# Turning table with its zero amid the chunks, output maps without power 0, and a new order of the S5 steps

## The chip, the cores and the metric

The kernel runs on one core of one Trainium2 chip. The metric is the device time of one execution in microseconds (us), from launch to the end; the number that counts is the median of several runs.

## What is computed

The reference is one step of a small hybrid encoder: two layers over 512 prompt rows and 32 sample rows of width 1024. Both layers end in a gated convolutional FFN. The change concerns the mixer of the first layer, an S5 state-space branch beside a cross-attention into 256 memory tokens:

```python
def s5_mixer(u, h0_re, h0_im, a_re, a_im, log_dt, b_re, b_im, c_re, c_im, d_skip, w_glu, b_glu):
    ...
    lam_re, lam_im = mag * jnp.cos(a_im * dt), mag * jnp.sin(a_im * dt)
    ...
    bu_re = jnp.einsum('blgc,gnc->blgn', ug, bb_re)
    bu_im = jnp.einsum('blgc,gnc->blgn', ug, bb_im)
    ...
    _, _, h_re, h_im = lax.associative_scan(
        _complex_affine_combine, (lam_re_t, lam_im_t, bu_re, bu_im), axis=1)
    y = (jnp.einsum('blgn,gcn->blgc', h_re, c_re.astype(f32))
         - jnp.einsum('blgn,gcn->blgc', h_im, c_im.astype(f32)))
    y = y.reshape(Bsz, L, MIX_IN) + d_skip.astype(f32) * u.astype(f32)
    y = jax.nn.gelu(y).astype(u.dtype)
    out = y * jax.nn.sigmoid(y @ w_glu + b_glu)
    return out, h_re[:, -1], h_im[:, -1]
```

There are 48 groups of 16 channels with 64 complex states each. The memory attention takes q from the same input gemm, normalises it over 64 columns, and attends to keys and values that a gemm over the memory tokens (prompt) or a cache (sample) gives.

## The kernel before

The kernel is one program with a fixed order on each of the five engines. Its blocks are written as Python functions, some as generators that are advanced by `unit(name, generator)`. A scheduler takes each block's instructions with a priority from the table ORDER (L63), and what comes out is the order in which each engine works, in sequence. Tiles come from free lists (Slots): a step that gets a tile waits until its last reader is done.

Large gemms are all in L324: fp32 operands split into a high and a low part, weights fetched by SP (L230), split by ACT into whi and wlo (L231, L232), and the low part is made by an accumulating DMA that POOL issues (L233).

The first layer goes through these stages, with times of the profile before:

- up to 69 us the input gemm (z0, L324 with ra and w_in), with the parameters of the S5 branch computed beside it in `s5_params`;
- from 69 to about 171 us the S5 stage in six chunks of 8 groups (128 channels);
- from 171 to 209 us the glu gemm (w_glu) with the memory attention between its six column blocks; then the rest of the kernel.

In the S5 stage eight time steps form a block, so that a sequence is 64 blocks (and 4 for the sample rows). For each chunk m:

- `s5_wv` (L671 on) makes on DVE the products that map inputs to states (L674, L676), `s5_wvt` transposes them on PE (L685);
- `s5_wc` (L693 on) makes on DVE the products of c and the powers of lambda (two L698 and their sum L700, each 128 x 1152: 8 groups, 9 powers, 16 channels). Powers 0 to 7 go with xq through 8 matmuls into the bank pk (L704), ACT evicts it into kp (L710), POOL adds the skip diagonal dd (L709, L711) and writes the block to DRAM (kd, L714);
- `s5_kernel` (L717 on) reads it back by eight DMAs of POOL (L723), each as a Toeplitz matrix, into two tiles kk;
- `s5_input` transposes the inputs of the chunk (PE L733, ACT L735, PE L743, ACT L744);
- `s5_scan` (L749 on) multiplies by wv on PE (L756), turns the phase by the table tab on DVE (L767 to L771), runs the real recurrence as a scan (L774; its factors `mul` and input `w` are prepared by ACT L760 and by the POOL memsets L761 and L763), turns back (L777), and forms hh (L783, L784). The table has 70 columns for each of 24 pairs of rows, real and imaginary part: powers 0 to 64 of the unit phase, and the columns 65 to 69 for the sample rows. It is built in `s5_params` by doubling (L640 to L650);
- `s5_output` multiplies u by kk (L795) and hh by powers 1 to 8 of wc (L796), evicts (ACT L800), transposes (PE L807), and applies the gelu (ACT L808, L809).

The loop over chunks (L1045 on) runs scan m, then the input and the products of chunk m+1, the output of chunk m-1, and at its end do_wc(m+1). Between them `fill` puts units of `mem_kv` (L337 on, matmuls L347), the gemm over the memory tokens, whose inputs have two tiles "rb" of their own. The memory attention `mem_attend` is a generator; its first part, norms of q and the sample rows' attention, runs ahead of the glu loop, and the others at blocks 1, 2, 4 and 5.

In the orders and rows below, rc is the split input of a gemm, bank a PSUM bank, fa, fx and big are tiles of the free lists (fx and big join late), and i_ names are inputs in DRAM.

Of the kernel before, what the change touches and what calls it, by code (L numbers as in the profile page):

```python
# [50 lines left out]
for _n, _w in (("mix", 2 * KD), ("bglu", NM), ("ffn", 2 * KD), ("kv", KD), ("mem", 2 * KD), ("ql", NM),  # L51
# [12 lines left out]
         "s5_input": 260, "norm0": 20, "s5_params": -50, "mem_attend0": 100, "s5_wc": 10, "q_front0": 10, "norm1": 0,  # L64
# [73 lines left out]
def body(ctx, tc, A, O):  # L138
# [5 lines left out]
    FW = 576  # L144
# [39 lines left out]
    warm = F.get(576)  # L184
# [3 lines left out]
    for _ in range(2):  # L188
        T.matmul(b, warm[:, 64:192], warm[:, 64:], start=True, stop=True)
# [227 lines left out]
    def mem_attend(l, zm, kv_p, kv_s, fm, bm, out):  # L417
        ktp, vp = kv_p
        kts, vs = kv_s
# [21 lines left out]
        r = rsqrt(x, 128, 17, "zr")  # L441
        mx, nm, su, ri = (sm(17, n) for n in ("zmx", "znm", "zsu", "zri"))
# [101 lines left out]
    def s5_params(pool, tmp, sp5):  # L544
# [121 lines left out]
        P.memset(q["kp"], 0.0)  # L666
        q["hf"] = pool.tile([128, NM, 8, 2], F32, name="hf")
# [377 lines left out]
    for m in range(NM):  # L1045
# [759 lines left out]
```

## Time and profile before

| what | before |
| --- | --- |
| median of 3 runs | 1437.56 us (1436.07 to 1439.15) |
| the profiled execution | 1436.17 us |
| its span, first to last instruction | 1434.4 us |
| PE busy | 1402.3 us (98%) |
| DVE busy | 714.6 us (50%) |
| ACT busy | 740.6 us (52%) |
| POOL busy | 385.7 us (27%) |
| mean granted clock of TensorE | 0.988 |

PE is the tensor engine, DVE the vector engine, ACT the scalar engine, POOL the general one, SP the one that issues DMAs. A busy PE can still work at half its clock: the column PEclk says which share of full speed was granted in a stretch. Idle time of the other engines costs nothing as long as PE does not wait for it. In the views, "[1.34 <-DVE wv L676]" behind a row says how long the engine stood before it and what released it.

### The profile page before, as it was taken

What the parts mean: (1) busy time and instruction counts of PE and PEld (TensorE: products, weight loads), DVE (VectorE), ACT (ScalarE), POOL (GpSimd) and SP (SyncE); (2) the same over time, 40 slices, a digit from 0 to 9 for tenths busy, and PEclk for the clock granted to TensorE, in tenths of its full rate; (3) what the DMA queues carried; (4) which work ended last, traced back from release to release, by engine and by line L of the source; (5) the groups of instructions that cost most, each with busy time, mean ns of one, the idle gap of its engine ahead of it and who ended that gap; (6) DMA issues with size and microseconds to landing.
All of it is one profiled execution on the core that took longest, in us unless ns stands there. A gap on an engine that the chain in (4) does not pass through costs nothing.

```text
span 1434.4 us, 26764 instructions
## 1 busy us (share of the span) xinstructions
PE 1402.3 (98%) x10661; PEld 1299.2 (91%) x10661; DVE 714.6 (50%) x1776; ACT 740.6 (52%) x1237; POOL 385.7 (27%) x668
## 2 busy tenths in 40 slices
PE   7999899999999999999989999999999999999998
PEld 6966689999999999999978986558999999999998
DVE  7999642555315541555357545663455514551351
ACT  6556464655435543555644554654565534553452
POOL 2065333222111211133336222332322211221121
PEclk8999899999999999999999999999999999999999
DMA  9443548788788888868741521103778887888775
GB/s 268 109 118 104 151 109 190 161 173 180 171 175 175 175 175 175 176 145 196 154 118 56 158 71 45 30 1 74 170 169 176 176 177 173 176 175 177 171 157 140
DMA packets 66045, 210.59 MB, mean 147 GB/s; under 512 B 9152, under 2 KB 11424, under 8 KB 65920
## 3 DMA queue, kind: packets, MB, share of 16 engines
q0 software_dynamic: 29152, 96.61, 37.4%
q1 hardware_dynamic: 35616, 110.17, 26.6%
q10 hardware_dynamic: 1152, 2.10, 0.4%
q8 instruction: 84, 1.38, 0.4%
q14 instruction: 41, 0.34, 0.1%
HBM read 203.22 MB, written 5.61 MB: 146 GB/s over the span
## 4 chain that ended last, share of the span: by engine, by line
PE 87%; DMA 4%; DVE 3%; ACT 2%; issue 2%; POOL 1%; SPq 0%; ACTq 0%; DVEq 0%; POOLq 0%
PE bank L324 67%; PE bank L1312 2%; PE bank L1560 2%; PE bank L1399 2%; PE bank L1596 1%; DMA wlo<-i_w_in 1%; PE bank L1513 1%; PE bank L1487 1%; PE bank L1585 1%; PE bank L347 1%; DMA wlo<-i_w_f 1%; PE bank L1201 1%; PE bank L479 1%; PE bank L1427 1%; PE bank L517 1%
## 5 line engine op out<-in xcount | busy, mean ns | idle before, releaser
L324 PE MATMUL bank<-rc,whi 128*128 128x272 f32 x3728 | 625.3, 289 | 0.2 <-DVE rc L305 0.2
L324 PEld LDWEIGHTS bank<-rc,whi 128*128 128x128 f32 x3728 | 528.2, 188 | 4.2 <-issue 3.1
L324 PE MATMUL bank<-rc,wlo 128*128 128x272 f32 x1864 | 388.3, 288 | 0.5 <-DMA wlo<-i_w_in 0.3
L231 ACT ACTIVATE whi<-wraw 128x1024 fp32r<-128x1024 f32 (+2 forms) x178 | 182.9, 1028 | 354.3 <-issue 304.0
L324 PEld LDWEIGHTS bank<-rc,wlo 128*128 128x128 f32 x1864 | 293.2, 188 | 1.3 <-DMA wlo<-i_w_in 0.5
L324 PE MATMUL bank<-g,whi 128*128 128x272 f32 x1408 | 234.8, 288 | 0.8 <-ACT g L216 0.8
L324 PEld LDWEIGHTS bank<-g,whi 128*128 128x128 f32 x1408 | 198.9, 188 | 1.4 <-ACT g L216 1.2
L233 POOL DMA_DIRECT2D wlo<-i_w_f x136 | 116.7, 858 | 303.9 <-ACT wlo L232 302.5
L232 ACT ACTIVATE wlo<-wraw 128x1024 fp32r<-128x1024 f32 (+2 forms) x178 | 180.6, 1015 | 0.6 <-PE bank L1513 0.5
L324 PE MATMUL bank<-g,wlo 128*128 128x272 f32 x704 | 145.6, 288 | 2.1 <-DMA wlo<-i_w_f 2.1
L855 DVE SCALAR_TENSOR_TENSOR fa<-fa,gp,fa 128x546 f32<-128x546 f32 x88 | 69.6, 791 | 139.6 <-ACT fa L854 139.6
L869 DVE TENSOR_TENSOR h<-bank,h 128x272 f32<-128x272 f32 x96 | 38.2, 435 | 173.2 <-PE bank L324 172.6
L324 PEld LDWEIGHTS bank<-g,wlo 128*128 128x128 f32 x704 | 110.3, 188 | 2.5 <-DMA wlo<-i_w_f 2.5
L854 ACT ACTIVATE fa<-fa,gp 128x546 f32<-128x546 f32 x88 | 73.1, 831 | 12.5 <-DVE fa L849 12.5
L847 DVE TENSOR_TENSOR fa<-bank,fa 128x272 f32<-128x272 f32 x88 | 38.9, 442 | 80.5 <-PE bank L324 76.7
L856 DVE SCALAR_TENSOR_TENSOR fa<-fa,gp,fa 128x546 f32<-128x546 f32 x88 | 69.5, 790 | 3.1
L895 ACT ACTIVATE fa<-fa 128x546 f32<-128x546 f32 x44 | 29.1, 662 | 71.7 <-DVE fa L856 71.7
L851 POOL COPY fa<-gp 128x2 f32<-128x2 f32 x88 | 19.9, 227 | 170.2 <-DVE g L217 107.9
L852 POOL COPY fa<-fa 128x4 f32<-128x4 f32 x88 | 18.2, 207 | 164.5 <-DVE fa L849 164.5
L324 PE MATMUL bank<-ra,whi 128*128 128x272 f32 x256 | 47.7, 309 | 2.7 <-ACT whi L241 2.7
L216 ACT ACTIVATE g<-fa 128x544 fp32r<-128x544 f32 x44 | 28.9, 658 | 37.6 <-DVE fa L897 37.6
L896 DVE TENSOR_TENSOR fa<-fa,fa 128x512 f32<-128x512 f32 x44 | 30.5, 693 | 33.5 <-ACT fa L895 33.5
(628 smaller groups left out, 1987.2 us busy)
## 6 DMA issues: line engine op xcount, KB each, us to landing
wraw<-i_w_f SPq DMA_DIRECT2D x120, 512.0 KB, 4.9
wlo<-i_w_f POOLq DMA_DIRECT2D x120, 512.0 KB, 7.4
wraw<-i_w_out SPq DMA_DIRECT2D x16, 512.0 KB, 4.4
wlo<-i_w_out POOLq DMA_DIRECT2D x16, 512.0 KB, 7.0
wraw<-i_w_in SPq DMA_DIRECT2D x14, 512.0 KB, 5.1
wlo<-i_w_in POOLq DMA_DIRECT2D x14, 512.0 KB, 7.5
wraw<-i_w_f SPq DMA_DIRECT2D x16, 384.0 KB, 3.1
wlo<-i_w_f POOLq DMA_DIRECT2D x16, 384.0 KB, 5.9
```

The lines of the kernel that those rows point to most:

```text
L216: S.activation(hi, src, AF.Copy)
L231: S.activation(hi, raw, AF.Copy)
L232: S.activation(lo, raw, AF.Copy, scale=-1.0)
L233: P.dma_start(lo, ap, accum_op=ALU.add)
L324: T.matmul(ps[q][:, :c], ww, xx[:, c0:c0 + c], start=k == 0 and i == 0, stop=k == n - 1 and i == 2)
L847: V.tensor_tensor(u[:, 2:274], ps[0][:, :272], rb[:, :272], ALU.mult)
L854: S.activation(y, u[:, 2:548], AF.Identity, scale=gcol("cw", 3 * ci + 2), bias=gcol("cb", ci))
L855: V.scalar_tensor_tensor(y, u[:, 1:547], gcol("cw", 3 * ci + 1), y, ALU.mult, ALU.add)
L856: V.scalar_tensor_tensor(y, u[:, 0:546], gcol("cw", 3 * ci), y, ALU.mult, ALU.add)
L869: V.tensor_tensor(h[m][:, c0:c0 + cc], ps[qd][:, :cc], h[m][:, c0:c0 + cc], ALU.add)
L895: S.activation(yg, yg, AF.Silu)
L896: V.tensor_tensor(u[:, 2:514], ya[:, :NP], yg[:, :NP], ALU.mult)
```

## The change

The table tab gets its zero turn at column 32 of 70. Powers 0 to 32 are built by doubling in six levels where there were eight; the 32 columns to the left are two reversed copies by ACT, the imaginary one with sign -1. A scan turned by a constant phase more or less gives the same states, so nothing else of it changes. The products wc hold powers 1 to 8 alone (128 x 1024), and power 0 of the kernel block comes from cc by a matmul of its own (16 columns, L710) beside that of powers 1 to 7 (112 columns, L711). The skip diagonal is computed once for all chunks (L670). do_wc(m+1) stands behind scan m and its first fill. mem_attend yields after the norms of q; that part runs in iteration 3 of the loop, the others at glu blocks 1 to 5, with priority 30 for the name mem_attend0 where 100 stood. FW goes from 576 to 560, the tiles tb and wc from 1152 columns to 1024, the two tiles rb of mem_kv fall away (it takes from F), and the order in which two tile sets join F is swapped.

```diff
-         "s5_input": 260, "norm0": 20, "s5_params": -50, "mem_attend0": 100, "s5_wc": 10, "q_front0": 10, "norm1": 0,
+         "s5_input": 260, "norm0": 20, "s5_params": -50, "mem_attend0": 30, "s5_wc": 10, "q_front0": 10, "norm1": 0,
...
-    FW = 576
+    FW = 560
...
         r = rsqrt(x, 128, 17, "zr")
+        if early:
+            yield
+        (ktp, vp), (kts, vs) = kv_p, kv_s() if early else kv_s
...
-        for o, lvl, c0, n in ((1, 0, 0, 1), (2, 1, 0, 2), (4, 2, 0, 4), (8, 3, 0, 8), (16, 4, 0, 16), (32, 5, 0, 16),
-                              (48, 5, 16, 16), (64, 6, 0, 1)):
+        for o, lvl, c0, n in ((1, 0, 0, 1), (2, 1, 0, 2), (4, 2, 0, 4), (8, 3, 0, 8), (16, 4, 0, 16), (32, 5, 0, 1)):
...
-        V.tensor_copy(view(tab, [[70, 2 * NPR], [1, 5]], 65), view(tab, [[70, 2 * NPR], [1, 5]]))
-
-        prd = pool.tile([128, 2, 9, 48], F32, name="prd")
+        for i, s in ((0, 1.0), (1, -1.0)):
+            S.activation(tab[:, i, :, 0:32], view(tab, [[70, NPR], [-1, 32]], SR * i + 64), AF.Copy, scale=s)
+        S.activation(view(tab, [[70, 2 * NPR], [1, 5]], 65), view(tab, [[70, 2 * NPR], [1, 5]], 32), AF.Copy)
+
+        prd = pool.tile([128, 2, 8, 48], F32, name="prd")
...
+        q["dd"] = pool.tile([128, 2 * NM, 16], F32, name="dd")
+        P.tensor_tensor(q["dd"], view(cn, [[0, 2 * NM], [1, 16]], 128), view(q["dsk"], [[1, 2 * NM], [0, 16]]), ALU.mult)
...
-        c, d = fd.get(8, 9, 16), fb.get(8, 9, 16)
+        c, d = fd.get(8, 8, 16), fb.get(8, 8, 16)
...
-                T.matmul(pk[32 * i:32 * i + 32, 128 * gh:128 * gh + 128],
-                         view(q["xq"], [[1, 32]], 16 * (8 * m + 4 * gh + i)),
-                         c[:, 4 * gh + i, 0:8].rearrange("p a b -> p (a b)"), start=True, stop=True)
+                x, g = view(q["xq"], [[1, 32]], 16 * (8 * m + 4 * gh + i)), 4 * gh + i
+                o = pk[32 * i:32 * i + 32, 128 * gh:128 * gh + 128]
+                T.matmul(o[:, :16], x, q["cc"][:, 0, 8 * m + g], start=True, stop=True)
+                T.matmul(o[:, 16:], x, c[:, g, 0:7].rearrange("p a b -> p (a b)"), start=True, stop=True)
...
-    R, fx = slots(lr, 2, F32, 512, "rb"), slots(lr, 3, F32, FW, "fx")
-    FA, FB, FD = slots(lr, 2, F32, 1024, "wv"), slots(lr, 1, F32, 2 * FW, "tb"), slots(lr, 3, F32, 2 * FW, "wc")
+    fx = slots(lr, 3, F32, FW, "fx")
+    FA, FB, FD = slots(lr, 2, F32, 1024, "wv"), slots(lr, 1, F32, 1024, "tb"), slots(lr, 3, F32, 1024, "wc")
     fxs = list(fx.free)
+    F.merge(Slots([big[:, FW * i:FW * i + FW] for i in range(4)]))
     F.merge(fx)
-    F.merge(Slots([big[:, FW * i:FW * i + FW] for i in range(4)]))
...
-    mkv = mem_kv(F, R, BG, BS, (kvp, (mk1, mv1)))
+    mkv = mem_kv(F, F, BG, BS, (kvp, (mk1, mv1)))
...
         fill(fills[m][0])
         if m < NM - 1:
+            do_wc(m + 1)
             g_in = s5_input(zts[m + 1], F, BS)
...
-        if m < NM - 1:
-            do_wc(m + 1)
+        if m == 3:
+            unit("att_norms", att)
...
-        if m in (1, 2, 4, 5):
+        if m:
             unit("mem_attend0", att)
```

What this does to the engines' orders is shown at three places. The first is POOL at the start, beside the input gemm. Before:

```order
L242 TENSOR_TENSOR wlo_100<-wraw_94,whi_97 128x512
L709 TENSOR_TENSOR fa_76<-cn,sp_145 128x32
L233 DMA wlo_101<-i_w_in 128x1024
L763 MEMSET fa_72 128x8
L233 DMA wlo_99<-i_w_in 128x1024
L233 DMA wlo_100<-i_w_in 128x1024
L761 MEMSET fa_79 128x8x2
```

After:

```order
L242 TENSOR_TENSOR wlo_100<-wraw_94,whi_97 128x512
L670 TENSOR_TENSOR dd<-cn,sp_145 128x192
L765 MEMSET fa_79 128x8
L233 DMA wlo_101<-i_w_in 128x1024
L233 DMA wlo_99<-i_w_in 128x1024
L233 DMA wlo_100<-i_w_in 128x1024
L763 MEMSET fa_78 128x8x2
```

The memset of the first scan's w moved from behind the first of the three weight DMAs to ahead of it, and its tile is another one.

The second place is DVE around the products of wc for the last chunk (wc_868 before, wc_862 after). Before, they stand behind the hh of scan 4 (L783, L784) and ahead of scan 5 (L767):

```order
L676 TENSOR_TENSOR wv_864<-wv_864,tb_865 128x1024
L783 TENSOR_TENSOR big<-fa_91,fa_86 64x280
L784 TENSOR_TENSOR big<-fa_91,fa_86 64x280
L783 TENSOR_TENSOR big<-fa_91,fa_86 64x280
L784 TENSOR_TENSOR big<-fa_91,fa_86 64x280
L698 TENSOR_TENSOR wc_868<-cc_399,prd 128x1152
L698 TENSOR_TENSOR tb_865<-cc_399,prd 128x1152
L217 TENSOR_TENSOR rc_1767<-fa_80,rc_1766 128x544
L700 TENSOR_TENSOR wc_868<-wc_868,tb_865 128x1152
L767 TENSOR_TENSOR fa_74<-bank_63,tab 128x4x69
```

After, they stand among the hh of scan 3 (L785, L786), and scan 4 (L769) begins ten rows behind these:

```order
L702 TENSOR_TENSOR wc_862<-cc_399,prd 128x1024
L785 TENSOR_TENSOR fa_92<-fa_75,fa_78 64x280
L786 TENSOR_TENSOR fa_92<-fa_75,fa_78 64x280
L785 TENSOR_TENSOR fa_92<-fa_75,fa_78 64x280
L786 TENSOR_TENSOR fa_92<-fa_75,fa_78 64x280
L702 TENSOR_TENSOR tb_859<-cc_399,prd 128x1024
L678 TENSOR_TENSOR wv_858<-bb_395,pr_397 128x1024
L704 TENSOR_TENSOR wc_862<-wc_862,tb_859 128x1024
L436 TENSOR_SCALAR zx_0_1479<-bank_70 128x17
L678 TENSOR_TENSOR tb_859<-bs_396,pi_398 128x1024
```

The products of the last chunk moved one scan forward, and the norms of q (L436) came in behind them.

The third place is POOL around the last kernel block (kd_394) and its reload. Before:

```order
L763 MEMSET fx_860 128x8
L355 TENSOR_TENSOR fx_862<-fx_862,fa_79 128x512
L233 DMA wlo_101<-i_w_glu 128x768
L711 TENSOR_TENSOR kp<-kp,big 128x2x16
L714 DMA kd_394<-kp 128x480
L430 MEMSET fa_73 128x256
L723 DMA fa_92<-kd_394 128x1x128 x4
L723 DMA fa_72<-kd_394 128x1x128 x4
L233 DMA wlo_99<-i_w_glu 128x768
```

After:

```order
L788 COPY hf<-fa_92 128x16
L714 TENSOR_TENSOR kp<-kp,dd 128x2x16
L716 DMA kd_394<-kp 128x480
L355 TENSOR_TENSOR big<-big,fa_78 128x512
L725 DMA fa_74<-kd_394 128x1x128 x4
L725 DMA fx_856<-kd_394 128x1x128 x4
L788 COPY hf<-fa_79 128x16
L763 MEMSET big 128x8x2
L765 MEMSET fa_91 128x8
L233 DMA wlo_101<-i_w_glu 128x768
```

The block's write and reload moved ahead of the memsets of the last scan and of the first weights of the glu gemm.

## Rows read from the trace of the kernel before

**Rows 1.** Windows: stretch, length; busy PE, PEld, DVE, ACT, POOL; PEclk, DMA share, GB/s

```profile
69.00:140.00 71.00, 66.76 (x608) 46.79 (x607) 68.62 (x100) 39.02 (x101) 42.87 (x73) 0.98 0.37 109
140.00:150.00 10.00, 9.42 (x66) 6.15 (x64) 8.87 (x27) 3.13 (x7) 3.68 (x5) 1.00 0.67 175
150.00:160.00 10.00, 5.61 (x27) 4.69 (x28) 6.04 (x23) 5.91 (x16) 7.95 (x13) 0.61 0.66 136
160.00:171.38 11.38, 11.24 (x62) 7.29 (x60) 5.19 (x24) 6.89 (x17) 1.73 (x3) 0.80 0.45 159
```

**Rows 2.** Waits of PE, 69 to 171.38 us: released by; total us, times, longest

```profile
PE bank L795 <- DMA fa<-kd: 2.5, 2, 1.7
PE bank L807 <- ACT big L800: 2.5, 1, 2.5
PE bank L685 <- DVE wv L676: 1.3, 1, 1.3
...
PE bank L704 <- DVE wc L700: 0.7, 1, 0.7
```

**Rows 3.** Chain that ended last, at the S5 stage's end: start, us, what

```profile
144.18 6.59 DMA kd<-kp
...
151.66 4.71 DMA fa<-kd
```

**Rows 4.** Timeline of DVE: start, us, line, out<-in [idle before <-releaser]

```profile
124.73 0.45 DVE L767 TENSOR_TENSOR fa<-bank,tab 128x276 f32<-128x276 f32 x1
...
139.19 1.35 DVE L700 TENSOR_TENSOR wc<-wc,tb 128x1152 f32<-128x1152 f32 x1
...
150.33 0.45 DVE L784 TENSOR_TENSOR fa<-fa,fx 64x280 f32<-64x280 f32 x1
```

**Rows 5.** Groups of DVE by form, 69 to 140 us: count, busy us, mean ns

```profile
L698 DVE TENSOR_TENSOR tb<-cc,prd 128x1152 f32<-128x1152 f32 x5 | 6.8, 1351 | 0.0
...
L674 DVE TENSOR_TENSOR tb<-bs,pi 128x1024 f32<-128x1024 f32 x4 | 4.9, 1226 | 0.0
```

**Rows 6.** Timeline of ACT near the S5 stage's end

```profile
150.16 0.84 ACT L231 ACTIVATE whi<-wraw 128x768 fp32r<-128x768 f32 x1 [3.46 <-DMA wraw<-i_w_glu]
```

**Rows 7.** Timeline of DVE, a table level of 16 columns

```profile
53.61 0.96 DVE L646 TENSOR_TENSOR big<-tab,p_sc 128x768 f32<-128x768 f32 x1
54.48 0.95 DVE L647 TENSOR_TENSOR big<-tab,p_sc 128x768 f32<-128x768 f32 x1
...
56.62 0.55 DVE L648 TENSOR_TENSOR tab<-big 128x384 f32<-128x384 f32 x1
57.09 0.55 DVE L649 TENSOR_TENSOR tab<-big 128x384 f32<-128x384 f32 x1
```

**Rows 8.** Timeline of PE, small matmuls

```profile
23.11 0.24 PE L262 MATMUL bank<-cn,fa 128*32 128x1 f32 x8
23.29 0.39 PE L324 MATMUL bank<-ra,whi 128*128 128x272 f32 x1
...
71.82 0.65 PE L704 MATMUL bank<-wc,xq 128*32 128x128 f32 x16
```

**Rows 9.** DMA issues of the whole run: count, KB each, us to landing

```profile
kd<-kp POOLq DMA_DIRECT2D x6, 240.0 KB, 2.4
...
fa<-i_mem SPq DMA_DIRECT2D x3, 256.0 KB, 2.9
```

**Rows 10.** Groups of ACT by form, 155 to 175 us

```profile
L376 ACT ACTIVATE fa<-bank,mrs 128x256 f32<-128x256 f32 x2 | 1.0, 496 | 1.9 <-PE bank L347 1.9
```

**Rows 11.** Timeline of DVE and PE at the front

```profile
19.98 0.72 DVE L953 TENSOR_TENSOR fa<-fa,fa 128x544 f32<-128x544 f32 x1
...
27.20 0.82 PE L324 MATMUL bank<-ra,wlo 128*128 128x272 f32 x2 [3.14 <-DMA wlo<-i_w_in]
```

**Rows 12.** The chain at the front

```profile
19.26 7.89 DMA wlo<-i_w_in
```

**Rows 13.** Timeline of PE in the glu stage

```profile
187.80 0.66 PE L507 MATMUL bank<-cn,fa 128*128 128x128 f32 x4 [1.08 <-POOL fa L495]
```

More of the change, by code (lines that the diff above doesn't have):

```diff
@@ L183, in body @@
     h = [base.tile([128, NT], F32, name=f"h{k}") for k in range(KD)]
-    warm = F.get(576)
+    warm = F.get(560)
     V.memset(warm, 0.0)
@@ L188, in body @@
     for _ in range(2):
-        T.matmul(b, warm[:, 64:192], warm[:, 64:], start=True, stop=True)
+        T.matmul(b, warm[:, :128], warm[:, :512], start=True, stop=True)
     B.put(b)
@@ L414, in mem_cache, with mem_attend @@
         return kt, v
-    def mem_attend(l, zm, kv_p, kv_s, fm, bm, out):
-        ktp, vp = kv_p
-        kts, vs = kv_s
+    def mem_attend(l, zm, kv_p, kv_s, fm, bm, out, early=False):
         ps = bm.get(512)
@@ L637, in s5_params @@
         tab = pool.tile([128, 2, NPR, 70], F32, name="tab")
-        V.memset(tab[:, 0, :, 0:1], 1.0)
-        V.memset(tab[:, 1, :, 0:1], 0.0)
+        V.memset(tab[:, 0, :, 32:33], 1.0)
+        V.memset(tab[:, 1, :, 32:33], 0.0)
         SR = NPR * 70
-        for o, lvl, c0, n in ((1, 0, 0, 1), (2, 1, 0, 2), (4, 2, 0, 4), (8, 3, 0, 8), (16, 4, 0, 16), (32, 5, 0, 16),
-                              (48, 5, 16, 16), (64, 6, 0, 1)):
+        for o, lvl, c0, n in ((1, 0, 0, 1), (2, 1, 0, 2), (4, 2, 0, 4), (8, 3, 0, 8), (16, 4, 0, 16), (32, 5, 0, 1)):
             t0 = view(tmp, [[NPR * n, 2], [n, NPR], [1, n]])
             t1 = view(tmp, [[NPR * n, 2], [n, NPR], [1, n]], H)
-            src = view(tab, [[SR, 2], [70, NPR], [1, n]], c0)
+            src = view(tab, [[SR, 2], [70, NPR], [1, n]], 32 + c0)
             V.tensor_tensor(t0, src, view(sc, [[0, 2], [1, NPR], [0, n]], NPR * (lvl + 1)), ALU.mult)
             V.tensor_tensor(t1, src, view(sc, [[0, 2], [1, NPR], [0, n]], NPR * (8 + lvl + 1)), ALU.mult)
-            V.tensor_tensor(tab[:, 0, :, o:o + n], t0[:, 0], t1[:, 1], ALU.subtract)
-            V.tensor_tensor(tab[:, 1, :, o:o + n], t0[:, 1], t1[:, 0], ALU.add)
-        V.tensor_copy(view(tab, [[70, 2 * NPR], [1, 5]], 65), view(tab, [[70, 2 * NPR], [1, 5]]))
-        prd = pool.tile([128, 2, 9, 48], F32, name="prd")
+            V.tensor_tensor(tab[:, 0, :, 32 + o:32 + o + n], t0[:, 0], t1[:, 1], ALU.subtract)
+            V.tensor_tensor(tab[:, 1, :, 32 + o:32 + o + n], t0[:, 1], t1[:, 0], ALU.add)
+        for i, s in ((0, 1.0), (1, -1.0)):
+            S.activation(tab[:, i, :, 0:32], view(tab, [[70, NPR], [-1, 32]], SR * i + 64), AF.Copy, scale=s)
+        S.activation(view(tab, [[70, 2 * NPR], [1, 5]], 65), view(tab, [[70, 2 * NPR], [1, 5]], 32), AF.Copy)
+        prd = pool.tile([128, 2, 8, 48], F32, name="prd")
         xq = pool.tile([128, 49, 16], F32, name="xq")
@@ L795, in s5_output @@
                 T.matmul(o, u[:, 4 * gh + i, :], kk[gh][:, i], start=True, stop=False)
-                T.matmul(o, hh[:, 4 * gh + i, 0:69], wc[:, 4 * gh + i, 1:9].rearrange("p a b -> p (a b)"), start=False,
+                T.matmul(o, hh[:, 4 * gh + i, 0:69], wc[:, 4 * gh + i].rearrange("p a b -> p (a b)"), start=False,
                          stop=True)
@@ L1023, in fill @@
             nfill += 1
-    wvs = []
+    wvs, mo = [], []
+    att = mem_attend(0, zm, kvp, lambda: kvs, F, BS, mo, True)
     def products(m):
```

16 lines of the change are left out of this document (5 added, 11 removed).

## Prediction

> **What bounds the kernel now.** The profile's page gives PE 98% of the span, so a gain can only come from where PE stands still or runs slowly. The windows show where that is [rows 1]. From 69 to 140 us PE is busy 66.76 of 71.00 us at a clock of 0.98; the next ten are nearly full (9.42); from 150 to 160 us it is busy 5.61 of 10.00 at clock 0.61, and up to 171.38 us it is busy but at 0.80. Behind that lie the glu gemm and work that the change doesn't touch: behind the glu stage every engine's order is word for word the same. So the question is when the glu gemm starts, 171.38 us now.
>
> The list of waits says what PE stood on between 69 and 171.38 us [rows 2]: 2.5 us on the loads of the last chunk's Toeplitz tiles (DMA fa<-kd), 2.5 us on an ACT eviction (L800), 1.3 us on DVE's products (wv), 0.7 us on DVE's wc. The chain explains the first two [rows 3]: the last kernel block is written to DRAM at 144.18 us, lands 6.59 us later, and its reload takes 4.71 us more; the reload releases PE. The block is late because it is computed late: DVE ends the products of wc for chunk 5 at 140.54 us (139.19 + 1.35), after scan 4, and the last hh is ready at 150.78 (150.33 + 0.45) [rows 4]. Through the whole S5 stage it is DVE that sets the pace: 68.62 busy of 71.00 us [rows 1].
>
> The change acts on these two things, DVE's amount of work and the place of the wc step, and it adds small work on PE and moves waits on POOL and ACT.
>
> **A. The tail (minus 9.4).** do_wc(m+1) goes from the end of an iteration to right behind scan m. In DVE's order the three wc operations of chunk 5 leave the place behind scan 4 and stand with the hh of scan 3. From wc to reloaded tile takes 15.83 us now (140.54 to 156.37, [rows 3, 4]). In the new order scan 4 and scan 5 lie in between. From the first operation of scan 4 (124.73) to the last hh (150.78) are 26.05 us now [rows 4], of which the three wc operations that leave are 4.0 (1351 ns each, [rows 5]), so some 22 us are left and the reload lands 6 us before hh needs it, even at the slow 6.59. The 2.5 us on DMA then go. The 2.5 us on L800 go too: L800 stood on ACT behind an L231 that waited 3.46 us for its weights at 150.16 us [rows 6]; in ACT's new order the L231 of the first two glu weights stand ahead of the evictions of chunk 4, not between those. That makes 5.0 us of waits. The clock is priced from the windows: (1 - 0.61) x 5.61 + (1 - 0.80) x 11.24 = 2.2 + 2.2 = 4.4 us [rows 1], lost in a stretch in which PE stood still again and again; what still waits behind the last hh I count under D. Ends: 0 (the reload comes late all the same) and -9.4. I take -9.4.
>
> **B. DVE's work (minus 5.7).** The table loses two levels of 16 columns: four products at a step of 0.87 us (53.61 to 54.48) and four sums at 0.47 (56.62 to 57.09), 5.4 us [rows 7]. The 18 wc operations shrink from 1152 to 1024 columns: L698 takes 1351 ns and L674, the same kind on 1024, 1226 [rows 5], 18 x 0.125 = 2.3. Together -7.7; the table's copy of five columns goes to ACT besides. Added ahead of the last hh is the query norm (eight operations on 17 columns and some copies: about 2 us, a guess, since the trace has them later and in the shadow of other work), so DVE is 5.7 us shorter. What this can give PE is what PE stood on in 69 to 150 us: 71.00 - 66.76 + 10.00 - 9.42 = 4.8 us, and (1 - 0.98) x 66.76 = 1.3 of clock, 6.1 [rows 1]. The smaller counts, -5.7. Ends 0 and -6.1. The two reversed copies of the table on ACT (128x768) lie beside the z0 gemm; without that cover they hold up the first scan, by no more than DVE's 0.87 for as many columns each [rows 7].
>
> **C. PE's new matmuls (plus 1.8).** Power 0 no longer lies in wc, so each of the 48 kernel products becomes two: 16 columns from cc and 112 from wc. L704's sixteen records, two for each product, take at most 0.65 us, 41 ns each; eight records of one column (L262) take 0.18 us (23.11 to 23.29), 22.5 ns each [rows 8]. 96 new records lie between 96 x 0.0225 = 2.2 and 96 x 0.041 = 3.9 us; the old ones lose an eighth, 0.4. So 1.8 to 3.5; sixteen columns are nearer to one than to 128, and I take 1.8. The Trainium skill (TensorE: Matmul & The Clock Gate, section "Wait — 56ns, not 53.3ns?") has starts never closer than about 25 ns however few the columns; the trace goes slightly below it with 22.5, and the measurement decides. By the skill's figure the term would be 2.0, an estimate from that page, and the sum -5.6.
>
> **D. New waits in fixed orders (plus 6.0).** The trace of before can't show these; I followed each engine's new order row by row with the durations of old rows. (1) kp is one tile, and chunk 1's eviction now waits until chunk 0's block was read by its DMA: the write lands in 2.4 us [rows 9], ACT is there about 1.5 us after its issue, 0.9. (2) PE's order has the kernel products of wc for chunk 3 ahead of transposes that are ready, and DVE is not done with them: 1.6, against 1.3 for the like stall on wv today [rows 2]. (3) The mem_kv inputs lose their own two tiles and share those of the scans, so the second block's load waits for scan 1 and takes 2.9 us [rows 9], of which other matmuls cover half: 1.5. (4) Behind the last hh, ACT has the L802 of chunk 5 behind six evictions of mem_kv (L376, L377) that wait for DVE's norm: 6 x 0.496 = 3.0 [rows 10], a third of it while PE still multiplies: 2.0. Ends: 0 (filler matmuls L347 lie in all of them) and 10 (each costs half as much again in PE's slow clock, as 160 to 171.38 us shows).
>
> **E. The front (plus 1.5).** POOL's first memset of the scan, L765, now stands ahead of the first L233 of these weights, and its tile is last read by DVE's L953 at 19.98, done 20.70 [rows 11]. The L233 was issued at 19.26, its data took 7.89 us [rows 12] and released PE at 27.20 after a stand of 3.14 us; the chain runs through it. Issued 1.5 us later (20.70 and the memset itself, against 19.26) it lands as much later: +1.5. The other side: the two L233 behind it come earlier than today (the second stood behind a memset that waited for PE), so nothing else is late, 0; or they share the queues with the first, three transfers instead of two, 7.89 / 2 = 3.9 more. The nearest row is the load itself, and I take 1.5. The diagonal's product (L670, one for six) ends before and is free.
>
> **Edits at nothing.** The attention units move within the glu stage, whose only notable stand is 1.08 us at 187.80 us on POOL's L495 [rows 13]; it comes later in the new order by 13 gemm matmuls of 216, which hide the same work: 0, ends -1.3 and +1.5. Smaller tiles and the new order of free lists cost nothing beyond D.
>
> Sum: -9.4 - 5.7 + 1.8 + 6.0 + 1.5 = -5.8 us. The profiled execution took 1436.17 us, 1434.4 of it the span; the change would give 1430.4. The median stands 1.4 above it: 1437.56 - 5.8 = 1431.8 us, 0.4% faster.
>
> **The rivals.**
> 1. *PE is simply full.* Filler matmuls cover all of D, which then gives 0: 1431.8 - 6.0 = 1425.8 us. For it: the 32 matmuls of mem_kv (L347) are fillers. Against it: stalls remain today in spite of them [rows 2]. 0.24.
> 2. *DVE's time goes elsewhere.* What DVE saves is eaten by waits on PE's and ACT's order, and the last hh comes at 150.8 as today, so that B is 0: 1437.56 - 9.4 + 1.8 + 6.0 + 1.5 = 1437.5 us, no change. For it: DVE starts the stage only when PE's z0 gemm ends at 69 us, and what it can do earlier is bounded by free tiles. 0.18.
> 3. *The reload is late again.* The eight loads of chunk 5 wait, on POOL's in-order queue, for tiles that scan 4 reads last (fa_74 by PE, fx_856 by DVE's scan). If these come more than 6 us later than in A, PE stands on the loads as today and A is 0: 1437.56 - 5.7 + 1.8 + 6.0 + 1.5 = 1441.2 us, slower. For it: POOL has eight issues of 0.6 us in a row. Against it: the 6 us of slack. 0.08.
>
> **How the numbers follow.** Forecast 0.50, the rivals 0.24, 0.18 and 0.08. About 0.2% or 2.9 us is what a measurement of this kernel can tell from no change: 1434.7 to 1440.4. The forecast and rival 1 are faster (0.74), rival 2 is the same (0.18), rival 3 slower (0.08). The range leaves out rival 3 and little below rival 1: 1424.5 to 1438.0; the forecast's own part of it is 1428 to 1435.
>
> **What would show it.** Right: no wait of PE on fa<-kd; the write of the last block issued before the last hh; the last hh at about 145 us instead of 150.78; the glu gemm starting some 9 us earlier (part of the attention's matmuls now lies behind its start), with clock 0.9 or more in the 20 us before it. E shows as PE's first stand ending at about 28.7 instead of 27.20. Wrong: a hh at 150 us or later (rival 2), loads that land behind it (rival 3), or a z0 gemm that ends later than 71 us.

## The result, and the profile after

The changed kernel is slower: a median of 1456.11 us (1453.64 to 1461.6, four runs) beside 1438.19 us (1436.07 to 1439.15, four runs) for the kernel before, a ratio of 1.0132 with a 95% interval of 1.0099 to 1.0165. The prediction was 1431.8 us in a range of 1424.5 to 1438.0, so it missed in size and in sign.

| what | before | after |
| --- | --- | --- |
| the profiled execution, its span | 1436.17, 1434.4 us | 1453.64, 1451.9 us |
| z0 gemm, its last matmul starts | 68.75 | 67.83 |
| last hh of scans 0 to 5 ready | 82.3, 93.3, 107.6, 124.7, 136.0, 150.8 | 81.4, 90.7, 110.2, 125.7, 146.7, 165.5 |
| glu gemm starts | 171.38 | 171.62 |
| length of the glu stage (from the first of its 216 matmuls of L324 to the next L324 behind them, with the attention between) | 44.41 | 55.78 |
| from there to the 600th L324 (in the gemm with w_out) | 47.93 | 54.39 |

The two profiled executions are 17.5 us apart. The glu stage is 11.4 us longer and the stretch behind it 6.5: together all of it (behind the gemm with w_out the kernel after is 0.6 us shorter). At the start of the glu gemm, the point on which the prediction argued, the two kernels are level, and neither gain nor loss is left there. But level hides two things: the last scan ends 14.7 us later than before, and some work of the attention has gone behind the start of the glu gemm.

The windows of the kernel after (stretch, length; busy PE, PEld, DVE, ACT, POOL; PEclk, DMA share, GB/s) answer to [rows 1]:

```profile
69.00:120.00 51.00, 46.53 (x511) 33.05 (x512) 44.30 (x70) 25.35 (x65) 26.26 (x53) 1.00 0.38 110
120.00:130.00 10.00, 6.53 (x31) 3.86 (x30) 9.04 (x14) 6.09 (x16) 5.71 (x11) 0.85 0.33 96
130.00:140.00 10.00, 10.00 (x100) 6.64 (x98) 5.67 (x15) 3.07 (x7) 1.21 (x3) 0.81 0.21 67
140.00:150.00 10.00, 8.90 (x63) 6.48 (x62) 6.50 (x15) 4.11 (x14) 6.16 (x12) 1.00 0.45 132
150.00:160.00 10.00, 8.98 (x74) 6.01 (x73) 4.11 (x8) 6.12 (x15) 2.45 (x2) 1.00 0.44 107
160.00:171.62 11.62, 9.49 (x66) 6.77 (x65) 9.84 (x41) 8.64 (x25) 3.16 (x5) 1.00 0.70 187
...
230.00:240.00 10.00, 6.23 (x42) 6.01 (x41) 1.51 (x3) 4.33 (x6) 2.50 (x3) 0.81 0.93 214
240.00:250.00 10.00, 10.00 (x71) 10.00 (x70) 0.79 (x2) 2.55 (x3) 1.94 (x2) 0.85 0.50 119
```

The hole that the kernel before has at 150 to 160 us (5.61 busy at clock 0.61) is gone. A new one lies at 120 to 130 (6.53 at 0.85, with 0.81 in the ten behind it). DVE, which had 68.62 of 71.00 us to do, now idles: in the 91 us from 69 to 160 it is busy 69.6 us (83.5 before). And there is a hole at 230 us, far behind the stage of the prediction.

The waits of PE (68 to 171.62 us: released by; total us, times, longest) answer to [rows 2]:

```profile
PE bank L809 <- ACT fa L746: 2.7, 1, 2.7
PE bank L809 <- ACT fa L802: 1.8, 2, 1.0
PE bank L797 <- ACT kp L713: 1.3, 1, 1.3
```

No wait on the Toeplitz loads (fa<-kd) is left, as A said. L809 and L802 are the transposes and the eviction of s5_output, L746 the eviction of the transposed inputs u, L797 the matmul of u with the Toeplitz tiles. The waits of DVE in the same stretch:

```profile
DVE fa L769 <- PE bank L758: 10.4, 4, 5.6
DVE zx L436 <- PE bank L434: 3.6, 1, 3.6
```

L769 is the first operation of a scan on DVE, L758 the matmuls ahead of it. The scans now wait 10.4 us for PE; in the kernel before the corresponding wait was 0.7 us. L436 is the norm of q, brought forward by the change: DVE stands 3.6 us for its matmul in the middle of the stage.

### The profile page after: what moved, and what is told of

Same layout as the page of the kernel before. It is cut to its first block, busy times and chain, and to the rows that moved or that the text cites. A ratio compares the mean times of both kernels' runs of the same rounds, so it can differ in the third digit from the quotient of the medians.

```text
span 1451.9 us, 26946 instructions
## 1 busy us (share of the span) xinstructions
PE 1413.5 (97%) x10757; PEld 1300.7 (90%) x10757; DVE 708.2 (49%) x1767; ACT 742.7 (51%) x1240; POOL 374.7 (26%) x663
## 3 DMA queue, kind: packets, MB, share of 16 engines
q10 hardware_dynamic: 1152, 2.10, 0.4%
HBM read 203.22 MB, written 5.61 MB: 144 GB/s over the span
## 4 chain that ended last, share of the span: by engine, by line
PE 85%; DMA 4%; DVE 4%; issue 3%; ACT 2%; POOL 1%; SPq 0%; DVEq 0%; POOLq 0%; ACTq 0%
PE bank L324 65%; PE bank L1313 2%; PE bank L1561 2%; PE bank L1400 2%; DMA wlo<-i_w_in 1%; PE bank L1597 1%; PE bank L1514 1%; PE bank L347 1%; PE bank L1488 1%; PE bank L480 1%; PE bank L1586 1%; PE bank L1202 1%; DMA wlo<-i_w_f 1%; PE bank L518 1%; PE bank L1428 1%
## 5 line engine op out<-in xcount | busy, mean ns | idle before, releaser
L324 PE MATMUL bank<-rc,whi 128*128 128x272 f32 x3728 | 629.4, 289 | 0.8 <-ACT fa L811 0.6
L324 PEld LDWEIGHTS bank<-rc,whi 128*128 128x128 f32 x3728 | 531.1, 189 | 8.3 <-issue 6.2
L324 PE MATMUL bank<-rc,wlo 128*128 128x272 f32 x1864 | 391.8, 291 | 4.1 <-DMA wlo<-i_w_out 3.8
L324 PEld LDWEIGHTS bank<-rc,wlo 128*128 128x128 f32 x1864 | 293.2, 189 | 6.6 <-DMA wlo<-i_w_out 4.0
L324 PE MATMUL bank<-g,whi 128*128 128x272 f32 x1408 | 234.8, 289 | 0.8 <-ACT g L216 0.8
L324 PEld LDWEIGHTS bank<-g,whi 128*128 128x128 f32 x1408 | 198.6, 188 | 1.4 <-ACT g L216 1.2
L324 PE MATMUL bank<-g,wlo 128*128 128x272 f32 x704 | 145.6, 288 | 0.7 <-DMA wlo<-i_w_f 0.7
L324 PEld LDWEIGHTS bank<-g,wlo 128*128 128x128 f32 x704 | 110.5, 188 | 1.1 <-DMA wlo<-i_w_f 1.1
L324 PE MATMUL bank<-ra,whi 128*128 128x272 f32 x256 | 46.3, 302 | 2.4 <-DVE ra L305 1.3
L898 DVE TENSOR_TENSOR fa<-fa,fa 128x512 f32<-128x512 f32 x44 | 30.5, 693 | 33.5 <-ACT fa L897 33.5
```

The lines of the kernel that those rows point to most:

```text
L324: T.matmul(ps[q][:, :c], ww, xx[:, c0:c0 + c], start=k == 0 and i == 0, stop=k == n - 1 and i == 2)
L898: V.tensor_tensor(u[:, 2:514], ya[:, :NP], yg[:, :NP], ALU.mult)
```

## The experiments

All ratios are to the kernel before, run on the same chip in the same batch: its medians were 1439.76 us (beside e1 to e4), 1439.98 (e5 to e8) and 1439.51 (e9 to e12), 25 to 27 runs each. One kernel's runs spread by some 5 us to either side, so a stage of one profile is good to a few us; verdicts go by the ratios.

**e1: the priority alone undone.** The kernel after, with

```diff
-"mem_attend0": 30
+"mem_attend0": 100
```

> The changed kernel with the priority of mem_attend0 back at 100; nothing else. Theory P (the lower priority lets the scheduler cut the attention's matmuls into pairs and single ones between gemm matmuls, and each cut costs PE): up to the glu gemm all is as in the changed kernel (first glu matmul near 171.6 us), the 216 matmuls of the glu gemm and what lies between take about 47 us instead of 55.0 (the 43.7 of before plus some 3 us of attention work that the change moved behind the gemm's start), total about 1448. Rival M (the attention's work is in that stage whatever its priority): 54 to 55 us again, total 1456.

Measured: 1442.17 us, 1.0024 [1.0003, 1.0045]. One number in the scheduler's table carries 1.1 of the 1.3%, some 15 of the 18 us. What it does stands in the order of PE in the glu stage. With priority 100 the four matmuls L518 of one pass over keys, two pairs on the two halves of po, stand together:

```
805 L324 MATMUL bank_68<-rc_1838,wlo_100 128x272
806 L518 MATMUL bank_67<-fa_75,fa_90 64x512
807 L518 MATMUL bank_67<-fa_79,fa_90 64x512
808 L518 MATMUL bank_67<-fa_71,fa_90 64x512
809 L518 MATMUL bank_67<-fa_86,fa_90 64x512
810 L480 MATMUL bank_64<-fa_89,fa_88 128x256 x2
```

With priority 30, in the kernel after, the second pair is cut by matmuls of the gemm:

```
825 L324 MATMUL bank_68<-rc_1844,whi_97 128x272
826 L518 MATMUL bank_67<-fa_71,fa_90 64x512
827 L324 MATMUL bank_66<-rc_1844,whi_97 128x272
828 L324 MATMUL bank_68<-rc_1845,whi_97 128x272
829 L518 MATMUL bank_67<-fa_86,fa_90 64x512
830 L324 MATMUL bank_66<-rc_1845,whi_97 128x272
```

(The first pair stands together at rows 813 and 814; of the four matmuls of the next pass none stands beside another.) What a cut costs is in the timelines of PE (start, us; a matmul of this form leaves two records, so x8 are four matmuls). Before (there the line is L517), both passes:

```profile
189.20 1.94 PE L517 MATMUL bank<-fa,fa 128*64 128x512 f32 x8
...
207.07 1.94 PE L517 MATMUL bank<-fa,fa 128*64 128x512 f32 x8
```

After:

```profile
193.59 1.93 PE L518 MATMUL bank<-fa,fa 128*64 128x512 f32 x4
...
196.91 1.07 PE L518 MATMUL bank<-fa,fa 128*64 128x512 f32 x2
...
198.36 1.07 PE L518 MATMUL bank<-fa,fa 128*64 128x512 f32 x2
```

Four matmuls took 1.94 us when they stood together; two took 1.93, and one alone 1.07. Windows that grow from the start of the first run, before (only L517; length, busy PE with records, busy PEld with records, PEclk, DMA share, GB/s), show why:

```profile
189.20:189.40 0.20, 0.20 (x2) 0.20 (x4) 1.00 0.00 0
189.20:189.80 0.60, 0.60 (x4) 0.32 (x6) 1.00 0.00 0
```

Two records have begun within 0.20 us, four within 0.60: the two matmuls of a pair, each on 64 columns of the array, run side by side. The same of the first piece after (only L518):

```profile
193.59:193.80 0.21, 0.21 (x1) 0.19 (x2) 1.00 0.00 0
193.59:194.20 0.61, 0.61 (x2) 0.19 (x2) 1.00 0.00 0
```

Here they begin one by one, two within 0.61 us. This pair is uncut, but the second matmul comes late; the weight loads (PEld, after) say on what. Its load stood 0.66 us for L511, DVE's copy of the transposed probabilities that this matmul multiplies:

```profile
194.45 0.19 PEld L518 LDWEIGHTS bank<-fa,fa 128*64 128x64 f32 x2 [0.66 <-DVE fa L511]
```

So a pair gains only when its two halves are neighbours in PE's order and both ready. The Trainium skill (TensorEngine Tiling (Array Packing), section "Tiling Modes", Key Properties) says that different tiles of the array can run their matmuls in parallel, and that a change of the tiling mode drains the engine; the trace agrees with the first (four matmuls in the time of two). The second no run here shows: the 216 gemm matmuls of the stage took 33.8 us start to start after, with 90 changes between gemm and attention, and 30.5 before with 34; but in e3 they took 32.4 us, also with 34 changes, and in e10 33.8 with 48. No price of a change comes out of these.

The stage by classes of matmul, from the groups by form of PE (count; busy us, mean ns; idle before). Before:

```profile
L479 PE MATMUL bank<-fa,fa 64*128 64x256 f32 x26 | 5.5, 420 | 0.0
...
L517 PE MATMUL bank<-fa,fa 128*64 128x512 f32 x16 | 3.9, 605 | 0.0
```

After:

```profile
L480 PE MATMUL bank<-fa,fa 64*128 64x256 f32 x32 | 9.1, 428 | 0.0
L518 PE MATMUL bank<-fa,fa 128*64 128x512 f32 x16 | 8.4, 618 | 0.0
```

And e1:

```profile
L480 PE MATMUL bank<-fa,fa 64*128 64x256 f32 x32 | 8.3, 412 | 0.0
...
L518 PE MATMUL bank<-fa,fa 128*64 128x512 f32 x16 | 3.9, 605 | 0.0
```

The same 16 records of the probabilities by v take 3.9, 8.4 and again 3.9 us. A few records of L480 (26 before, 32 after) moved behind the gemm's start by the split itself and stay there in e1. The glu stage of e1 is 49.11 us against 55.78. Of these 6.7 us, counted from the start of each matmul to the next start on PE, 4.1 lie at L518, 2.1 at the gemm's own matmuls and 0.5 at L480.

The second half of the priority's price lies behind the glu stage and on another engine. POOL after, around the low parts of the w_out weights:

```profile
217.08 0.87 POOL L233 DMA_DIRECT2D wlo<-i_w_out  x1 [0.96 <-ACT wlo L232]
229.34 0.09 POOL L838 MEMSET fa<- 128x2 f32 x1 [11.39 <-DVE fa L1099]
...
229.92 0.87 POOL L233 DMA_DIRECT2D wlo<-i_w_out  x1 [0.35 <-issue]
```

In e1 the second of these loads stands ahead of the memset:

```profile
220.12 0.86 POOL L233 DMA_DIRECT2D wlo<-i_w_out  x1 [8.15 <-PE bank L324]
223.73 0.10 POOL L838 MEMSET fa<- 128x2 f32 x1 [2.75 <-DVE fa L1099]
```

The memset waits for the last product of the glu stage (DVE L1099), and a load that waits for nothing of the sort is queued behind it. PE, after, then stands on it:

```profile
237.85 0.82 PE L324 MATMUL bank<-rc,wlo 128*128 128x272 f32 x2 [3.77 <-DMA wlo<-i_w_out]
```

The granted clock is 0.81 and 0.85 in the twenty us around this stand, where it was 1.00 before. The stretch is 48.09 us long in e1 and 54.39 after.

**e2: the priority alone done.** The kernel before with 30 for 100.

> The kernel before with the priority of mem_attend0 at 30 instead of 100; nothing else. Theory P: the order of S5 stays as before, the glu stage grows from 43.7 us to 50 or more, total 1443 to 1446. Rival M: no change, 1438.

Measured: 1461.35 us, 1.0144 [1.0105, 1.0184]. The priority costs as much in the kernel before, some 15 us more than the expectation had. In its glu stage L479 is cut likewise (start to start 9.94 us where the kernel before has 4.69) and L517 in part (5.88 for 3.73), and PE stands on two weight loads, one within the glu gemm and the one of w_out:

```profile
201.49 0.52 PE L324 MATMUL bank<-rc,wlo 128*128 128x272 f32 x2 [4.18 <-DMA wlo<-i_w_glu]
...
245.96 0.82 PE L324 MATMUL bank<-rc,wlo 128*128 128x272 f32 x2 [4.67 <-DMA wlo<-i_w_out]
```

Its glu stage is 61.70 us long, at a clock of 0.84, the stretch behind it 54.81. The eleven kernels of the study with priority 100 (e1, e3 to e12) have no stand on w_out, and their stretch is 47.9 to 48.2 us long.

**e3: the split of the attention undone as well.** e1, with mem_attend created and its first part run ahead of the glu loop, the others at blocks 1, 2, 4 and 5:

```diff
-        if m == 3:
-            unit("att_norms", att)
...
+    att = mem_attend(0, zm, kvp, kvs, F, BS, mo)
+    unit("mem_attend0", att)
...
-        if m:
+        if m in (1, 2, 4, 5):
```

> The changed kernel with the attention undone: no early norms in the loop, units at blocks 1, 2, 4 and 5, priority 100. Theory S (the S5 stage of the changed kernel is slowed by its early wc step and shared tiles, the norms are a small part): the last hh stays near 163 us (165.5 in the changed kernel, 150.8 before), the glu gemm starts at 172 to 176 and takes 44 us, total 1440 to 1445. Rival N (the norms' 20 matmuls ahead of scan 4 are what delays it by 10 us): the last hh comes at about 152 to 155 us, the glu gemm starts before 168, total 1430 to 1436.

Measured: 1442.35 us, 1.0018 [0.9995, 1.0042]. Beside e1 the split by itself does nothing that can be measured: glu starts at 175.21 instead of 172.69, and the glu stage takes 46.61 instead of 49.11 us.

**e4: only do_wc moved, in the kernel before.**

```diff
         fill(fills[m][0])
         if m < NM - 1:
+            do_wc(m + 1)
...
-        if m < NM - 1:
-            do_wc(m + 1)
```

> The kernel before with do_wc(m+1) behind scan m and its first fill instead of at the iteration's end; table, wc, attention and tiles as before. Theory A (my term A): the reload of the last chunk is there when hh comes, PE's waits on fa<-kd and on L800 (5.0 us) go, with the clock 9.4: total 1429 to 1433. Rival S: with the wc step ahead of the next chunk's input, kernel products and reloads hold tiles and PE's order ahead of the next scan's products; the scans slip, the last hh comes later than 150.8 us, total 1438 or more.

Measured: 1445.82 us, 1.0037 [1.0014, 1.0061]. Alone, the move that term A rests on makes the kernel slower. No wait on fa<-kd is left in this trace either; instead DVE's waits, 69 to 173.8 us, read

```profile
DVE fa L767 <- ACT fa L687: 3.3, 1, 3.3
DVE fa L767 <- PE bank L807: 2.3, 1, 2.3
```

L687 evicts the transposed wv. In the new order the products of wc stand on DVE ahead of and among those of wv (the change's second order listing shows L702 ahead of L678). A scan needs wv at once and wc only at its output, so that what is wanted first comes later. The last hh is ready at 155.27 us, 4.5 later than before.

**e5: the computations of the change without its moves.** The kernel after with priority 100, do_wc at the end, the old attention, and the diagonal per chunk and the old order of joining F; what stays are the new table, power 0 out of wc and mem_kv's inputs in F.

> The changed kernel with its computations (table from the middle, wc without power 0, FW 560, mem_kv's inputs from the shared tiles) but with the order of before: do_wc at the iteration's end, attention units at blocks 1, 2, 4 and 5 with priority 100, the skip diagonal per chunk. Theory D (DVE sets the pace of S5, my terms B and C): the last hh comes 4 to 6 us earlier than 150.8, total 1432 to 1436. Rival Q (what DVE saves turns into waits on PE's fixed order): the last hh between 149 and 153 us with DVE idle for some 6 us more than before, total 1437 to 1441.

Measured: 1436.49 us, 0.9978 [0.9960, 0.9995]: on the faster side of the kernel before, just clear of it. Neither case foresaw the way: the last hh is ready only at 155.49 us, yet the glu gemm starts at 170.05, 1.3 us earlier than before.

**e6: only the two tiles of mem_kv taken away, in the kernel before.**

```diff
-    mkv = mem_kv(F, R, BG, BS, (kvp, (mk1, mv1)))
+    mkv = mem_kv(F, F, BG, BS, (kvp, (mk1, mv1)))
```

> The kernel before with mem_kv's inputs taken from the shared tiles instead of two of their own; nothing else. Theory T (shared tiles delay mem_kv's loads and so the scans behind its matmuls): the last hh 2 to 5 us later than 150.8, total 1440 to 1443. Rival: no change, 1438.

Measured: 1450.52 us, 1.0080 [1.0057, 1.0103]. No instruction is added; tiles are shared, and that alone costs some 11 us, where 2 to 5 had been expected. Its PE, 69 to 180.9 us, stands on two evictions:

```profile
PE bank L807 <- ACT fa L744: 4.0, 1, 4.0
PE bank L807 <- ACT fa L800: 3.4, 1, 3.4
```

**e7: do_wc back at the end, the early norms kept.** The kernel after with priority 100, do_wc, diagonal and joining as before.

> The changed kernel with do_wc back at the iteration's end and the priority at 100 (and the diagonal per chunk, the merge order of before, without which it doesn't fit); the norms of q still early. Beside the run of the changed kernel at priority 100 (1442) it is the wc step's place alone. Theory S (the early wc step delays the scans): the last hh at 150 to 155 us instead of 166, glu start near 167 to 170, total 1436 to 1439. Rival A (the early step gains): the kd wait of 5 us is back, total 1446 or more.

Measured: 1442.07 us, 1.0014 [0.9999, 1.0029]. With e1, e3 and e5 this makes a square: neither move 0.9978, only do_wc (with the diagonal and the joining) 1.0018, only the norms 1.0014, both 1.0024. Either one brings the whole loss of 0.4%, the second adds next to nothing. The place of do_wc is thus not alone what delays the scans: in e7, without it, the last hh is ready at 162.51 us, where the expectation had 150 to 155.

**e8: only power 0 out of wc, in the kernel before.** Tiles of 128 x 1024, the added matmul from cc, and nothing else:

```diff
+                T.matmul(o[:, :16], x, q["cc"][:, 0, 8 * m + g], start=True, stop=True)
+                T.matmul(o[:, 16:], x, c[:, g, 0:7].rearrange("p a b -> p (a b)"), start=True, stop=True)
```

> The kernel before with power 0 taken out of wc: 128x1024 products on DVE, 48 more small matmuls on PE; nothing else. By my prices DVE loses 2.3 us of work and PE gains 1.8: total 1437 to 1439 if the two cancel (theory C), 1440 or more if the small matmuls or the new order cost more (rival), 1436 or less if DVE's share alone counts.

Measured: 1432.98 us, 0.9951 [0.9931, 0.9971]: faster than both kernels, and the best of the study. The reload that PE waited for is early enough here without any move. POOL (write of the last block, then its loads; [rows 3] has 144.18 and 151.66):

```profile
142.74 0.59 POOL L715 DMA_DIRECT2D kd<-kp  x1 [0.30 <-POOL kp L712]
143.40 0.93 POOL L233 DMA_DIRECT2D wlo<-i_w_glu  x1
146.07 3.01 POOL L724 DMA_DIRECT2D fa<-kd  x5 [1.73 <-DMA kd<-kp]
```

In the kernel before, POOL has that weight load ahead of the write:

```profile
142.51 0.98 POOL L233 DMA_DIRECT2D wlo<-i_w_glu  x1 [0.83 <-ACT kp L710]
```

There the write took 6.59 us to land, here 3.0, so that it landed 5.0 us earlier though it was issued only 1.4 earlier. In the traces of all fourteen kernels the last write took 6.59 and 6.64 us in the two that have this load just ahead of it (before and e2) and 2.3 to 4.1 us in the other twelve. A run with the two issues swapped and nothing else was not made.

The windows of e8:

```profile
69.00:140.00 71.00, 68.16 (x695) 48.66 (x695) 69.85 (x104) 39.13 (x100) 40.78 (x73) 1.00 0.37 110
140.00:150.00 10.00, 10.00 (x90) 7.16 (x87) 8.69 (x27) 3.71 (x8) 7.14 (x12) 1.00 0.72 187
150.00:160.00 10.00, 9.10 (x64) 6.51 (x62) 7.78 (x29) 9.03 (x25) 4.95 (x8) 1.00 0.59 159
```

The hole at 150 us is closed and the clock is 1.00 throughout; glu starts at 163.70 us, 7.7 earlier than before. DVE still sets the pace (69.85 of 71.00), and the last hh is ready at 149.83, only 0.95 earlier: the gain is the tail, not DVE's pace.

**e9: e8 with do_wc moved** as in e4.

> The kernel with power 0 out of wc (the one that took 1433) with do_wc(m+1) behind scan m and its first fill besides; nothing else. Theory S (the early wc step delays the scans, as it did in the kernel before, by some 0.4%): last hh at 152 to 155 us instead of 149.8, total 1437 to 1441. Rival A (with the short wc the early step fits and adds its own gain): 1430 or less.

Measured: 1443.69 us, 1.0034 [1.0016, 1.0052], 0.8% above e8. Waits of DVE (69 to 176.4 us), the same two as in e4:

```profile
DVE fa L768 <- ACT fa L687: 3.7, 1, 3.7
DVE fa L768 <- PE bank L808: 3.5, 1, 3.5
```

The move's price shows on two bases; the last hh is ready at 158.51 us and glu starts at 176.38 us, 12.7 later than in e8.

**e10: e8 with the attention split and the norms early** (priority 100).

> The kernel with power 0 out of wc with the attention split besides (norms in iteration 3, units at blocks 1 to 5, priority 100). Theory N (the norms' matmuls and ACT steps in the loop and the cut attention cost some 0.4%): the glu stage takes 48 us or more instead of 44.8, total 1437 to 1441. Rival: 1431 to 1434, since the norms only change their place.

Measured: 1440.26 us, 1.0002 [0.9983, 1.0021], 0.5% above e8. Here the glu gemm starts as early as in e8 (163.02 us), and its stage is 55.76 us where e8 has 45.50. L518 runs whole (3.9 us); L480 takes 10.5 us for 32 records, and one of its stands, 2.2 us long, was released by ACT's tanh of the glu (L1098). Beside e3 the same edit cost nothing (e1); why it costs 0.5% here stays open:

```profile
L480 PE MATMUL bank<-fa,fa 64*128 64x256 f32 x32 | 10.5, 443 | 2.5 <-ACT fa L1098 2.2 <-ACT fa L451 0.4
```

**e11: e8 with mem_kv's inputs in F.**

> The kernel with power 0 out of wc, with mem_kv's inputs from the shared tiles. Theory T (sharing alone costs, 0.8% in the kernel before): 1441 to 1445, the last hh at 156 us or later, DVE standing 5 us or more on PE in one place. Rival (what the sharing costs depends on the rest): 1433 to 1437.

Measured: 1436.59 us, 0.9981 [0.9961, 1.0000]. The sharing costs 0.3% here, with an interval that nearly touches zero, against 0.8% in e6; with a shorter wc it hurts less.

**e12: the new table with mem_kv's inputs in F,** in the kernel before (with wc as it was).

> The kernel before with the table built from the middle and mem_kv's inputs from the shared tiles (with their own two tiles it doesn't fit). Against the same without the new table (1450): theory D, DVE's 5.4 us show as a last hh 4 to 6 us earlier than 158.5 and a total near 1445; rival, the table's time lies beside the z0 gemm, where PE is the bound, and nothing shows: 1450.

Measured: 1447.55 us, 1.0055 [1.0035, 1.0074]. Beside e6 (1.0080) the table may give 0.25%, with intervals that overlap, and the last hh comes 1.6 us earlier (156.94 for 158.49), not the 4 to 6 of the expectation; between e11 (0.9981) and e5 (0.9978) it gives nothing. That the table is worth much by itself was not seen. No run has the new table together with mem_kv's own two tiles.

**The way from before to after.** Each row adds one edit to the row above:

| kernel | adds | ratio to before | step |
| --- | --- | --- | --- |
| e8 | power 0 out of wc | 0.9951 | -0.49% |
| e11 | mem_kv's inputs in F | 0.9981 | +0.30% |
| e5 | new table, FW 560, narrower tb and wc tiles | 0.9978 | -0.03% |
| e3 | do_wc early, diagonal once, new joining | 1.0018 | +0.40% |
| e1 | norms early, attention split | 1.0024 | +0.06% |
| after | priority 30 | 1.0132 | +1.08% |

The ratios' intervals are some 0.2% to either side, that of after 0.33%. With the two half-widths of a step added in square, steps one, four and six stand clear of zero, and step two barely.

## Why the prediction was wrong

**Edits at nothing** is the step that failed. "The attention units move within the glu stage" was priced at 0 with ends of -1.3 and +1.5; it cost some 16 us (after against e3), of the two edits in it the priority nearly all (e1, e2). The reasoning looked at waits alone ([rows 13]: one stand of 1.08 us on POOL) and took the durations of the attention's matmuls as given. They are not: 16 records of one class took 3.9 or 8.4 us by their neighbours and by when their inputs came. The view that would have told it was at hand: in the order of PE the pairs are whole before and cut after, and the timeline has x8 in 1.94 us.

**"Behind the glu stage every engine's order is word for word the same"** was false, and the argument that only the start of the glu gemm counts rested on it. POOL's order has the memset L838 ahead of the second load of w_out instead of behind it. That is some 6 us: 3.8 of stand and the slow clock around it.

**A, the tail, minus 9.4.** Half right. The wait on fa<-kd did go, in the kernel after and in e4, and the last block is written long before its use. But the sign of the move was wrong: it delays the wv of the next chunk and costs 0.4% in e4 and 0.8% in e9. That a hole at 150 us could be closed was right, and e8 closes it with a wc that is a ninth shorter, without the move: 7.7 us in its profile, 7.0 by the medians (DVE's shorter products and PE's new matmuls included), against the 9.4 of the term. The cause that the term gives for the hole is the smaller part of it: of the 5.0 us by which the block lands earlier in e8, 1.4 come from its being computed earlier and 3.6 from a write that took 3.0 us instead of 6.59.

**B, DVE's work, minus 5.7.** The work did shrink, yet no time came of it: DVE's own waits in the stage grew instead, with 10.4 us on L758 in front. This is rival 2, which had been given 0.18, and worse than it: the last hh came at 165.5 us, not at the 150.8 that would have been its 0. Where the scans slip stands in the timelines. Scan 4, which began on DVE 0.03 us behind the hh of scan 3 before (124.73), begins 13.4 us behind it after (139.07): in between DVE makes the products wc and wv and stands 3.6 us for the norm's matmul. Scan 5 then waits for PE twice (DVE, after):

```profile
152.29 0.45 DVE L769 TENSOR_TENSOR fa<-bank,tab 128x276 f32<-128x276 f32 x1 [5.58 <-PE bank L758]
...
156.57 0.45 DVE L769 TENSOR_TENSOR fa<-bank,tab 128x276 f32<-128x276 f32 x1 [2.77 <-PE bank L758]
```

Between the two halves of L758 (151.48 and 155.76 us) PE's order has six records of mem_kv's gemm and some of the output of the chunk before:

```profile
152.12 2.84 PE L347 MATMUL bank<-wraw,fa 128*128 128x512 f32 x6
```

Scans that had run into each other on DVE now wait for places in DVE's and PE's orders. How much of it comes from each edit is not shown: without the early norms (e3 beside e1) the hh of scan 4 comes 5.3 us earlier, but the last hh only 2.4. Nor was the table's share where the term had it: its two levels stand at 53 to 61 us, beside the z0 gemm, and e12 gives 1.6 us at the last hh for them.

**C, PE's matmuls, plus 1.8.** In e8, which has all of them, the kernel is 7 us faster, so what they cost is covered. After, from 79.06 to 79.82 us, PE does the sixteen records of L710 and the fourteen in the trace of L711 of one chunk in 0.76 us (before, sixteen of L704 in at most 0.65, [rows 8]): 0.1 us a chunk, 0.7 in all by this row. (The 22.5 ns of the term is a mean: L262's eight records start some 7 ns apart in two groups of four, on strips of 32 columns.)

**D, new waits, plus 6.0.** The four named waits exist in part: kp 1.3 us (0.9 foreseen), L347 on its inputs 0.7 (1.5), L802 1.0 behind the last hh (2.0); a wait of L710 or L711 on wc is not among PE's waits. They were the wrong list. The shared tiles were priced as one load that waits for scan 1; as an edit by itself the sharing costs 11 us (e6) or 4 (e8 to e11). In e6 the evictions wait for tiles of the scans (ACT stood 2.9 us for DVE's L783 ahead of L744, 3.2 for L774 ahead of L800), and PE behind them.

**E, the front, plus 1.5.** The mechanism ran as described and cost nothing. The chain, after:

```profile
20.21 0.11 POOL fa L765
...
20.47 6.73 DMA wlo<-i_w_in
...
27.24 2.86 PE bank L324 x11
```

The load was issued 1.2 us later and flew 1.16 us shorter than the 7.89 of [rows 12], and PE went on at 27.24 instead of 27.20. A flight time taken from one row carried the term.

Rival 3, the only one on the slow side, did not happen; the slow side came from a place that no case had.

## What to carry to other kernels

Before a change of priorities or of places is priced at nothing, look in the engine's order for groups that are cheap only together (matmuls on parts of the array that run side by side) and for loads in an in-order queue that fall behind a waiting instruction: both are visible without a run. A producer moved earlier delays what stood there; price what is wanted first. When an edit is a bundle, try its arithmetic alone: here one of the bundle's parts was worth 0.5%, and the moves around it took that back and more.

## What the runs showed of the hardware

Two matmuls on the two halves of the array run in the time of one if they stand next to each other and are both ready: four in 1.94 us, and 1.07 us for one alone. With 64 rows the same is seen for L480, after (a matmul leaves two records here too):

```profile
184.81 0.70 PE L480 MATMUL bank<-fa,fa 64*128 64x256 f32 x2
...
185.88 0.70 PE L480 MATMUL bank<-fa,fa 64*128 64x256 f32 x4
```

One matmul in 0.70 us and a pair in 0.70 us. Mixed with the gemm, the attention's matmuls thus cost up to twice their time, and a busy PE looks equally full in both cases: in the glu stage after it was busy 54.81 of 55.78 us at clock 1.00.
